# Placing four stores of the second layer and laying out two state arrays row by row, in a two-layer decoder step

## The chip, the cores and the metric

The kernel runs on one core of a Trainium2 chip. The metric is the device time of one execution in microseconds (us); the time before is the median of three runs. A profile of one execution gives, for each engine, when its instructions ran and what released them. Times inside the trace count from the start of its span.

## What is computed

One inference step of a two-layer decoder, for a prompt of 256 tokens and eight sample sequences of one token each; all 264 tokens share the weights. Cut to what matters here:

```python
def sb_pool_mixer(x, pos, past_kv, pool_prev, norm_g, w_in, pool_w, pool_scale, w_out):   # layer 1
    h = rmsnorm(x, norm_g)
    z = h @ w_in
    q, k, v, u = jnp.split(z, [C_WIDTH, 2 * C_WIDTH, 3 * C_WIDTH], axis=-1)
    ...
    new_kv = jnp.stack([k, v], axis=2)
    c_out = stick_breaking_attention(q, k_all, v_all, pos).reshape(B, T, C_WIDTH)
    d_out = pool_mixer(pool_prev, u, pos, pool_w, pool_scale)
    new_pool = jnp.concatenate([pool_prev, u], axis=1)[:, -POOL_STATE:]
    y = jnp.concatenate([c_out, d_out], axis=-1) @ w_out
    return x + y, new_kv, new_pool

def conv_ffn(x, prev, norm_g, w_gate, w_up, conv_w, conv_b, w_down):                       # both layers
    g_all = jnp.concatenate([prev, h @ w_gate], axis=1)
    gc = sum(conv_w[i] * g_all[:, i:i + T] for i in range(CONV_W)) + conv_b
    ...
```

Outputs besides the activations are the new keys and values (k1 and v1 in layer 1), the last 15 pooling inputs of the prompt (poolp) and of the eight samples (pools), and the convolution states. The pooling state of the samples comes in as 15 earlier rows of 512 features for each sequence; a sequence's new state is rows 1 to 14 of these and the new row.

## The kernel before

The features lie on the 128 partitions, the 264 tokens along the free axis. Every weight is cut into blocks of 128 x 128, packed in the order of use, and streamed from device memory in chunks: sixteen blocks, 1 MB, each. A chunk goes into one of three buffers of the pool `rawp` (tile `raw`, issued in `raw`, line 280, through `late`, line 274). `split` (line 292) turns each half chunk, eight blocks, into two operand tiles: `wh` by a copy on ScalarE (ACT, line 300) and the rest `wl` by a subtraction on VectorE (DVE, line 301). It does so three tiles ahead of TensorE (PE), in four buffers. `run` (line 306) then issues three matmuls for each block, 24 for a tile.

The phases follow each other: in0, out0, ff0, dn0 for layer 0, then in1, out1, ff1, dn1. Phase in1 (line 1079) has 128 blocks in the order u, q, k, v, four output tiles of eight blocks each. The other work of the layer hangs on it by block number: `blk(b, f)` calls `f` in the trace after block b. The places that matter:

- `norm1` at block 12, which sets the scale that the evacuations of in1 need; `pool_in` (lines 1022 to 1024) writes `U` and column 15 of `PALL`; `pool_sum` (line 1026) at block 33 copies the tail of `U` to `plp` on GpSimd (POOL, line 1028) and forms the window sums on DVE.
- Sixteen pages of the cached values, 256 KB each, are loaded two at a time from block 40 to block 96 (`drip_of(vload, 2)`); two pages share one tile `V`.
- `zs_score` (line 996) at block 72 multiplies the sample queries with the cached keys (tile `sc`); `stick` (line 958) makes weights of the scores, with two sigmoids on ACT (lines 962, 963) and a scan and a product on DVE (lines 964, 965), into tile `zs`; `zs_tr` (line 1002) at block 82 transposes `zs` on PE into `pP`.
- `z_qk` at blocks 80, 93, 105, 117 does the same for the prompt (tiles `Z`, `keep`, `w`), and `z_tr` at 91, 104, 116 transposes `w` into `pt`. `sample_av` at blocks 100 and 108 uses the `V` tiles (`pv`).

While `fixed[0]` is true, from line 1060 to line 1092, matmuls keep their order in the trace. Everything that goes through `late`, or is pinned with `keep_in_program_order`, also keeps it. All other instructions are placed by a scheduler, engine by engine. The orders of PE, DVE, ACT and POOL are the same in the kernel before and the changed one.

Every weight chunk and every page is issued by SyncE (SP), one after the other. SP waits for a transfer's buffer before it issues it, and what stands behind waits too. Its order in layer 1, from line 935 on, with chunk numbers, is before:

```text
PALL, pw, raw54, raw55, out_pools, out_poolp, V0 V0, raw56, V2 V2 V4 V4, raw57, V6 V6 V8 V8, raw58,
V10 V10, V12 V12, raw59, V14 V14, out_k1, raw60, raw61, out_v1, raw62, raw63
```

Each DMA signals on one of eight semaphores in turn, so that the ninth of a row waits for the first. `PALL` is `[P, 4, 8, 16]` on chip. The load fills its columns 0 to 14 (line 935), and the store `pools` takes columns 1 to 15 (line 1088): 4096 pieces of 60 bytes each way. The convolution state `CSTATE` is `[P, 2, NF, 2, NS]`; `conv_prep` (line 531) stores one of its two rows for each layer, `CSTATE[:, l, :, 1, :]` (line 538), in 2816 pieces of 32 bytes.

Of the kernel before, what the change touches and what calls it, by code (L numbers as in the profile page):

```python
# [9 lines left out]
F32 = mybir.dt.float32  # L10
# [4 lines left out]
ALU = mybir.AluOpType  # L15
# [3 lines left out]
P = 128  # L19
# [3 lines left out]
NS = 8  # L23
T = SEQ + NS
# [7 lines left out]
NF = DFF // P  # L32
# [14 lines left out]
NST = 15  # L47
# [41 lines left out]
def _pack_weights(w_in0, w_out0, w_in1, w_out1, gate, up, down):  # L89
    def blocks(w):  # L90
        kt, mt = w.shape[0] // P, w.shape[1] // P
        return w.reshape(kt, P, mt, P).transpose(2, 0, 1, 3).reshape(mt * kt, P, P), kt

    mats = {"in0": w_in0, "out0": w_out0, "in1": w_in1, "out1": w_out1}
    for l in range(2):
        mats[f"g{l}"], mats[f"u{l}"], mats[f"dn{l}"] = gate[l], up[l], down[l]
    base, kts, parts, n = {}, {}, [], 0
    for name, w in mats.items():
        b, kts[name] = blocks(w)
        base[name] = n  # L100
        parts.append(b)
        n += b.shape[0]
    allb = np.concatenate(parts)
    idx = []
    for ph, order in _PHASES:
        for (n_, t), k in order:
            if ph in _COLS:
                name, m = ph, _COLS[ph][n_] + t
            elif ph.startswith("ff"):
                name, m = n_ + ph[2], t  # L110
            else:
                name, m = ph, t
            idx.append(base[name] + m * kts[name] + k)
    out, o = [], 0
    for c in _CHUNKS:
        out.append(allb[np.array(idx[o:o + c])].transpose(1, 0, 2).reshape(-1))
        o += c
    return out
# [11 lines left out]
def _pack_first(gain, x, chunks):  # L130
    w = np.concatenate([c.reshape(P, -1) for c in chunks[:2]], 1)
    rows = []
    for i, ((b, e), (m, n)) in enumerate(_FIRST):
        rows.append(np.concatenate(([gain] if i == 0 else []) + [w[:, b * P:e * P], x[:, m:n].reshape(P, -1)], 1).reshape(-1))
    return np.concatenate(rows)
# [18 lines left out]
def _consts():  # L154
# [35 lines left out]
_INS = [  # L190
    ("w", ((_NB - 16) * P * P,)), ("xw", (P * (KD + 16 * P + KD * T),)), ("x", (P, KD * T)), ("vec", (P, _NVEC)), ("cst", _CST_ARR.shape), ("rope", (P, 2 * T)),
    ("kt0", (NPHYS, P, 512)), ("vp0", (NPHYS, P, 512)), ("kt1", (NPHYS, P, 512)), ("vp1", (NPHYS, P, 512)),
    ("cstate", (P, 2 * NF * 2 * NS)), ("pstate", (P, 4 * NS * NST)),
    ("sguw", (P, 512)), ("sgub", (P, 512)), ("poolw", (P, 512)),
]
_OUTS = [
    ("y", (KD, P, T)), ("k0", (P, 4, T)), ("v0", (P, 4, T)), ("bvn", (P, 4, NS)),
    ("k1", (P, 4, T)), ("v1", (P, 4, T)), ("poolp", (P, 4, NST)), ("pools", (P, 4, NS, NST)),
    ("cv0", (P, NF, 10)), ("cv1", (P, NF, 10)), ("cs0", (P, NF, NS)), ("cs1", (P, NF, NS)),
]  # L200

# [2 lines left out]
def tile_decoder_step(ctx: ExitStack, tc: tile.TileContext, a):  # L204
    nc = tc.nc
    v, s, g = nc.vector, nc.scalar, nc.gpsimd
# [16 lines left out]
    con = ctx.enter_context(tc.tile_pool(name="con", bufs=1))  # L223
# [8 lines left out]
    def f4(name, shape=(P, 4, T), dt=F32):  # L232
        return up.tile(list(shape), dt, tag="u", name=name)
# [11 lines left out]
    VEC = con.tile([P, _NVEC], F32, name="VEC")  # L245
    CST = con.tile([P, _CST_ARR.shape[1]], F32, name="CST")
    PT = con.tile([1, NS * NPG], I32, name="PT")
    CSTATE = con.tile([P, 2, NF, 2, NS], F32, name="CSTATE")
    C0 = con.tile([P, 2, NF, NS], F32, name="C0")
    PALL = con.tile([P, 4, NS, 16], F32, name="PALL")  # L250

# [4 lines left out]
    def vec(n):  # L256
        o, w = _VEC[n]
        return VEC[:, o:o + w]
# [15 lines left out]
    def late(dst, src):  # L274
        tc.keep_in_program_order(nc.sync.dma_start(dst, src))
# [30 lines left out]
    def run(order, rhs, evac, hooks=None):  # L306
        hooks = sorted((hooks or {}).items())
        n = 0
        seen, left, ps = {}, {}, {}
        for m, k in order:  # L310
            left[m] = left.get(m, 0) + 1
        for m, k in order:
            i = pos[0]
            pos[0] += 1
            h, l = split(i // 8)
            c = (i % 8) * P
            if m not in ps:
                ps[m] = at(f"mm{i}") if i in spare else psm.tile([P, 512], F32, tag="mm", name=f"mm{i}")
                first = True
            else:  # L320
                first = False
            left[m] -= 1
            o = ps[m][:, :T]
            xh, xl = rhs(m, k)
            pe.matmul(o, h[:, c:c + P], xh, start=first, stop=False)
            pe.matmul(o, h[:, c:c + P], xl, start=False, stop=False)
            pe.matmul(o, l[:, c:c + P], xh, start=False, stop=left[m] == 0)
            if left[m] == 0:
                evac(m, o)
            n += 1  # L330
            while hooks and n >= round(8 * (hooks[0][0] + 1)):
                for f in hooks.pop(0)[1]:
                    f()
# [11 lines left out]
    first, o = [], 0  # L345
# [185 lines left out]
    def conv_prep(l):  # L531
        cw = vec("cw")
        w = lambda i: cw[:, (l * 3 + i) * NF:(l * 3 + i + 1) * NF].unsqueeze(2).to_broadcast([P, NF, NS])
        t = sm.tile([P, NF, NS], F32, tag="cprep", name=f"cprep{l}", bufs=1)
        g.tensor_tensor(C0[:, l], CSTATE[:, l, :, 0, :], w(0), ALU.mult)
        g.tensor_tensor(t, CSTATE[:, l, :, 1, :], w(1), ALU.mult)
        g.tensor_tensor(C0[:, l], C0[:, l], t, ALU.add)
        nc.sync.dma_start(a[f"cs{l}"], CSTATE[:, l, :, 1, :])

    def ffn(l, xg, R, down_evac, hooks=None):  # L540
        cw, cb = vec("cw"), vec("cb")
# [61 lines left out]
    def pick(xg):  # L603
        return lambda m, k: hl(xg, k)
# [69 lines left out]
    q4, k4, v4 = f4("q4"), f4("k4"), f4("v4")  # L674
# [187 lines left out]
    blk = lambda b, f, *x: hk.at(b / 8 - 1, f, *x)  # L862
# [51 lines left out]
        blk(8, s_av, t)  # L914


    late(CSTATE, a["cstate"].rearrange("p (l j i s) -> p l j i s", l=2, j=NF, i=2))
    for l in range(2):
        conv_prep(l)

# [11 lines left out]
    ffn(0, xg, R, evac, hk)  # L932


    late(PALL[:, :, :, 0:NST], a["pstate"].rearrange("p (g s i) -> p g s i", g=4, s=NS))
    xg = xg1
    q4, k4, v4 = f4("q4b"), f4("k4b"), f4("v4b")
    vt = f4("vt1", (P, 2, 512))
# [3 lines left out]
    plp = sm.tile([P, 4, NST], F32, tag="plp", name="plp", bufs=1)  # L942
# [118 lines left out]
    blk = lambda b, f, *x: hk.at(b / 8 - 1, f, *x)  # L1061
# [7 lines left out]
        blk(b, z_qk, t)  # L1069
    for t, b in enumerate((91, 104, 116)):  # L1070
        blk(b, z_tr, t)
    blk(100, lambda: nc.sync.dma_start(a["k1"], k4))
    for i, b in enumerate((62, 66, 70, 76)):
        blk(b, pool_mix, i)
    for t, b in enumerate((110, 118, 126)):
# [1 line left out]
    for i, b in enumerate((100, 108)):  # L1077
        blk(b, sample_av_of(st1, PZ, vtiles, i, "l1"))
    run(orders["in1"], pick(xg), in1_evac, hk)
    nc.sync.dma_start(a["v1"], v4)  # L1080
    hk = Hooks()
    blk(1, zs_out)
    blk(2, z_tr, 3)
    blk(6, lambda: v_pair(vt, v4[:, 3, :], 3, "v1"))
    for t in range(4):
        blk(9, z_av, t)
    nc.sync.dma_start(a["poolp"], plp)
    nc.sync.dma_start(a["pools"], PALL[:, :, :, 1:16])

    xg, nrm, evac = residual(vec("f1"), "f1")  # L1090
    run(orders["out1"], pick([catA, catB]), evac, hk)
# [12 lines left out]
def _lay(inp):  # L1104
    f = {n: np.asarray(x) for n, x in inp.items()}
    x = np.concatenate([f["x_prompt"].reshape(SEQ, D), f["x_sample"].reshape(NS, D)])
    col = lambda w: w.reshape(-1, P).T
    kt = lambda c: c[:, :, 0].reshape(NPHYS, P, 4, P).transpose(0, 3, 2, 1).reshape(NPHYS, P, 512)
    vecs = {"n1": col(f["l1_norm"]), "f0": col(f["ffn_norm"][0]), "f1": col(f["ffn_norm"][1]),
            "fin": col(f["final_norm"]), "sg": col(f["l0_sgu_gain"]), "ps": col(f["l1_pool_scale"]),  # L1110
            "cw": col(f["ffn_conv_w"].reshape(-1)), "cb": col(f["ffn_conv_b"].reshape(-1)),
            "w00": np.tile(f["l0_sgu_w"][:, 0, 0][None, :], (P, 1)), "b00": np.tile(f["l0_sgu_b"][:, 0][None, :], (P, 1))}
    ws = _pack_weights(f["l0_w_in"], f["l0_w_out"], f["l1_w_in"], f["l1_w_out"], f["ffn_w_gate"], f["ffn_w_up"], f["ffn_w_down"])
    xt = x.T.reshape(KD, P, T).transpose(1, 0, 2)
    return {
        "w": np.concatenate(ws[2:]),
        "xw": _pack_first(col(f["l0_norm"]), xt, ws),
        "x": xt.reshape(P, KD * T),
        "vec": np.concatenate([vecs[n] for n in _VEC], 1),
        "cst": _CST_ARR,  # L1120
        "rope": _ROPE,
        "kt0": kt(f["cache_l0_kv"]), "vp0": f["cache_l0_kv"][:, :, 1].reshape(NPHYS, P, 512),
        "kt1": kt(f["cache_l1_kv"]), "vp1": f["cache_l1_kv"][:, :, 1].reshape(NPHYS, P, 512),
        "pt": f["page_table"].reshape(1, NS * NPG),
        "cstate": f["state_ffn_conv"].reshape(2, NS, 2, NF, P).transpose(4, 0, 3, 2, 1).reshape(P, -1),
        "pstate": f["state_l1_pool"].reshape(NS, NST, 4, P).transpose(3, 2, 0, 1).reshape(P, -1),
        "sguw": f["l0_sgu_w"].transpose(2, 0, 1).reshape(P, 512),
        "sgub": np.tile(f["l0_sgu_b"].reshape(1, 512), (P, 1)),
        "poolw": f["l1_pool_w"].transpose(1, 0, 2).reshape(P, 512),
    }  # L1130
# [39 lines left out]
```

## Time and profile before

| | us |
|---|---|
| time, median of 3 runs (lowest, highest) | 611.6 (610.9, 612.25) |
| the profiled execution | 612.44 |
| span of its trace | 610.3 |
| PE busy in the span | 593.2 |
| DVE, ACT, POOL busy | 417.4, 343.8, 66.7 |
| mean granted PE clock, share of full speed | 0.994 |

The profiled execution's own time is 2.14 us more than its span, and 0.84 us more than the median of the runs shown. PE is busy for 97% of the span, so a change in any other engine or queue shows in the time only where PE waits for it. Waits of an engine are listed with the instruction that ended them; "SPq" is SyncE's queue of DMA issues, and "landing" is the moment at which all of a transfer has arrived. "DMA" in a table of stretches is the busy share of the 16 DMA engines; it can be over 1, where packets overlap.

### The profile page before, as it was taken

Reading aid. Unit: us, or ns where it says so; the run is one execution under the profiler, and the core shown is the slowest. Engines: PE = TensorE matmul, PEld = TensorE weight load, DVE = VectorE, ACT = ScalarE, POOL = GpSimd, SP = SyncE. Lnnn points to the kernel's source line nnn. Section 1 sums busy time; section 2 is a strip of 40 time slices with the busy share of each in tenths; the row PEclk is TensorE's granted clock in tenths of the full one; section 3 lists DMA queues with packets and bytes.
Section 4 is the critical chain, followed back from the end, with each engine's and each line's share of the span. In section 5 each row is a group of like instructions: output and inputs, shape, how many; then the busy total and the mean of one; then the engine's idle time right before and its main releaser. Section 6 shows DMA issues by size and latency. Waiting matters only on the chain.

```text
span 610.3 us, 12279 instructions
## 1 busy us (share of the span) xinstructions
PE 593.2 (97%) x4908; PEld 573.3 (94%) x4908; DVE 417.4 (68%) x711; ACT 343.8 (56%) x607; POOL 66.7 (11%) x83
## 2 busy tenths in 40 slices
PE   8999999999999999999999799999999999999994
PEld 7988879999999999999999588999999999999994
DVE  6899566879776766655559276597986766754442
ACT  7757755576655555544454256566665555555441
POOL 4100002341000000011110000033300000001120
PEclk9999999999999999999999999999999999999998
DMA  8998936544654554894579992445365454564502
GB/s 324 347 396 293 333 123 173 200 147 139 213 202 164 182 205 150 333 333 166 201 178 86 262 356 106 169 154 198 133 214 177 169 207 158 189 209 154 199 1 71
DMA packets 41258, 122.23 MB, mean 200 GB/s; under 512 B 17138, under 2 KB 18546, under 8 KB 29810
## 3 DMA queue, kind: packets, MB, share of 16 engines
q1 hardware_dynamic: 40368, 120.25, 60.0%
q10 hardware_dynamic: 834, 1.20, 0.6%
q8 instruction: 38, 0.62, 0.4%
q14 instruction: 18, 0.15, 0.1%
HBM read 117.50 MB, written 3.94 MB: 199 GB/s over the span
## 4 chain that ended last, share of the span: by engine, by line
PE 71%; DVE 3%; DMA 2%; issue 1%; ACT 1%; POOL 0%; DVEq 0%; SPq 0%; ACTq 0%
PE mm L216 68%; DMA raw<-in_w 2%; DVE xn_l L386 1%; DVE wl L301 1%; PE pv_l L216 1%; PE Z L216 1%; PE pav L216 0%; DVE wk L565 0%; PE pt L219 0%; DVE X L1100 0%; DVE wk L566 0%; ACT wh L300 0%; POOL wk L576 0%; DVE wk L561 0%; PE vtp_v L219 0%
## 5 line engine op out<-in xcount | busy, mean ns | idle before, releaser
L301 DVE TENSOR_TENSOR wl<-raw,wh 128x1024 fp32r<-128x1024 f32 x179 | 220.4, 1231 | 132.7 <-ACT wh L300 130.8
L300 ACT ACTIVATE wh<-raw 128x1024 fp32r<-128x1024 f32 x179 | 189.6, 1060 | 184.4 <-PE mm L216 164.0
L216 PE MATMUL mm<-xn_h,wh 128*128 128x264 f32 x544 | 154.7, 284 | 0.0
L216 PE MATMUL mm<-xn_l,wh 128*128 128x264 f32 x544 | 154.5, 284 | 0.0
L216 PE MATMUL mm<-xn_h,wl 128*128 128x264 f32 x544 | 153.4, 282 | 0.0
L216 PEld LDWEIGHTS mm<-xn_h,wh 128*128 128x128 f32 x544 | 102.2, 188 | 0.2 <-ACT cvo L568 0.2
L216 PEld LDWEIGHTS mm<-xn_l,wh 128*128 128x128 f32 x544 | 102.2, 188 | 0.0
L216 PEld LDWEIGHTS mm<-xn_h,wl 128*128 128x128 f32 x544 | 102.2, 188 | 0.0
L216 PE MATMUL mm<-a_l,wh 128*128 128x264 f32 x352 | 99.8, 284 | 0.0
L216 PE MATMUL mm<-a_h,wh 128*128 128x264 f32 x352 | 99.7, 284 | 0.0
L216 PE MATMUL mm<-a_h,wl 128*128 128x264 f32 x352 | 99.3, 282 | 0.0
L216 PEld LDWEIGHTS mm<-a_l,wh 128*128 128x128 f32 x352 | 66.1, 188 | 0.0
L216 PEld LDWEIGHTS mm<-a_h,wl 128*128 128x128 f32 x352 | 66.1, 188 | 0.0
L216 PEld LDWEIGHTS mm<-a_h,wh 128*128 128x128 f32 x352 | 66.0, 188 | 0.0
L216 PE MATMUL mm<-xg_h,wh 128*128 128x264 f32 x160 | 48.2, 301 | 1.3 <-ACT xg_h L385 1.3
L216 PE MATMUL mm<-xg_f_h,wh 128*128 128x264 f32 x160 | 46.0, 288 | 2.0 <-DVE wk L575 2.0
L216 PE MATMUL mm<-xg_l,wh 128*128 128x264 f32 x160 | 46.2, 289 | 0.0
L216 PE MATMUL mm<-xg_h,wl 128*128 128x264 f32 x160 | 46.1, 288 | 0.0
L216 PE MATMUL mm<-xg_f_l,wh 128*128 128x264 f32 x160 | 45.4, 284 | 0.0
L216 PE MATMUL mm<-xg_f_h,wl 128*128 128x264 f32 x160 | 45.1, 282 | 0.0
L216 PE MATMUL mm<-xg_n_h,wh 128*128 128x264 f32 x128 | 39.2, 307 | 0.0
L216 PE MATMUL mm<-xg_n_l,wh 128*128 128x264 f32 x128 | 36.9, 288 | 0.0
(249 smaller groups left out, 1055.5 us busy)
## 6 DMA issues: line engine op xcount, KB each, us to landing
raw<-in_w SPq DMA_DIRECT2D x89, 1024.0 KB, 4.9
K<-in_kt SPq DMA_DIRECT2D x32, 256.0 KB, 6.1
V<-in_vp SPq DMA_DIRECT2D x32, 256.0 KB, 7.2
raw<-in_w SPq DMA_DIRECT2D x4, 512.0 KB, 5.8
X<-in_x SPq DMA_DIRECT2D x4, 264.0 KB
xw<-in_xw SPq DMA_DIRECT2D x2, 388.0 KB, 5.6
out_k<-k SPq DMA_DIRECT2D x1, 528.0 KB
out_v<-v SPq DMA_DIRECT2D x1, 528.0 KB
```

The costliest lines, as they stand in the source:

```text
L216: return self.keep(nc.tensor.matmul(*x, **k))
L300: s.activation(h, src, AF.Copy)
L301: v.tensor_tensor(l, src, h.bitcast(F32), ALU.subtract)
L386: j = v.scalar_tensor_tensor(l, src, gain, h.bitcast(F32), ALU.mult, ALU.subtract)
```

## The change

Four things are done. The stores of `poolp` and `pools` leave the trace's end of phase in1, where the scheduler placed them, and are held at block 84 of in1; the store of `k1` is held at block 112 instead of being a free one at block 100; the store of `v1` moves from the end of in1 to block 12 of out1, and is held there. The pooling state is given 16 columns for each sequence in device memory as well (the sixteenth is padding on the way in, and the first is dropped on the host on the way out), so that load and store move whole rows of 2 KB. The convolution state is laid out with its two rows outside the feature blocks, so that the row that is stored is contiguous: 704 bytes for each partition. SP's order in layer 1 after it:

```text
PALL, pw, raw54, raw55, V0 V0, raw56, V2 V2 V4 V4, raw57, V6 V6 V8 V8, raw58, V10 V10, out_poolp,
out_pools, V12 V12, raw59, V14 V14, raw60, out_k1, raw61, raw62, out_v1, raw63
```

```diff
-    ("cstate", (P, 2 * NF * 2 * NS)), ("pstate", (P, 4 * NS * NST)),
+    ("cstate", (P, 2 * NF * 2 * NS)), ("pstate", (P, 4 * NS * 16)),
...
-    ("k1", (P, 4, T)), ("v1", (P, 4, T)), ("poolp", (P, 4, NST)), ("pools", (P, 4, NS, NST)),
+    ("k1", (P, 4, T)), ("v1", (P, 4, T)), ("poolp", (P, 4, NST)), ("pools", (P, 4, NS, 16)),
...
-    CSTATE = con.tile([P, 2, NF, 2, NS], F32, name="CSTATE")
+    CSTATE = con.tile([P, 2, 2, NF, NS], F32, name="CSTATE")
...
-        g.tensor_tensor(C0[:, l], CSTATE[:, l, :, 0, :], w(0), ALU.mult)
-        g.tensor_tensor(t, CSTATE[:, l, :, 1, :], w(1), ALU.mult)
+        g.tensor_tensor(C0[:, l], CSTATE[:, l, 0], w(0), ALU.mult)
+        g.tensor_tensor(t, CSTATE[:, l, 1], w(1), ALU.mult)
         g.tensor_tensor(C0[:, l], C0[:, l], t, ALU.add)
-        nc.sync.dma_start(a[f"cs{l}"], CSTATE[:, l, :, 1, :])
+        nc.sync.dma_start(a[f"cs{l}"], CSTATE[:, l, 1])
...
-    late(CSTATE, a["cstate"].rearrange("p (l j i s) -> p l j i s", l=2, j=NF, i=2))
+    late(CSTATE, a["cstate"].rearrange("p (l i j s) -> p l i j s", l=2, i=2, j=NF))
...
-    late(PALL[:, :, :, 0:NST], a["pstate"].rearrange("p (g s i) -> p g s i", g=4, s=NS))
+    late(PALL, a["pstate"].rearrange("p (g s i) -> p g s i", g=4, s=NS))
...
-    blk(100, lambda: nc.sync.dma_start(a["k1"], k4))
+    blk(84, late, a["poolp"], plp)
+    blk(84, late, a["pools"], PALL)
+    blk(112, late, a["k1"], k4)
...
     run(orders["in1"], pick(xg), in1_evac, hk)
-    nc.sync.dma_start(a["v1"], v4)
     hk = Hooks()
     blk(1, zs_out)
     blk(2, z_tr, 3)
     blk(6, lambda: v_pair(vt, v4[:, 3, :], 3, "v1"))
     for t in range(4):
         blk(9, z_av, t)
-    nc.sync.dma_start(a["poolp"], plp)
-    nc.sync.dma_start(a["pools"], PALL[:, :, :, 1:16])
+    blk(12, late, a["v1"], v4)
...
-    pools = o["pools"].transpose(2, 3, 1, 0).reshape(NS, NST, 512)
+    pools = o["pools"][..., 1:].transpose(2, 3, 1, 0).reshape(NS, NST, 512)
```

More of the change, by code (lines that the diff above doesn't have):

```diff
@@ L1124, in _lay @@
         "pt": f["page_table"].reshape(1, NS * NPG),
-        "cstate": f["state_ffn_conv"].reshape(2, NS, 2, NF, P).transpose(4, 0, 3, 2, 1).reshape(P, -1),
-        "pstate": f["state_l1_pool"].reshape(NS, NST, 4, P).transpose(3, 2, 0, 1).reshape(P, -1),
+        "cstate": f["state_ffn_conv"].reshape(2, NS, 2, NF, P).transpose(4, 0, 2, 3, 1).reshape(P, -1),
+        "pstate": np.pad(f["state_l1_pool"].reshape(NS, NST, 4, P).transpose(3, 2, 0, 1), ((0, 0), (0, 0), (0, 0), (0, 1))).reshape(P, -1),
         "sguw": f["l0_sgu_w"].transpose(2, 0, 1).reshape(P, 512),
```

## The prediction

> **What bounds the kernel now.** I read the page first, for which engine is full.
>
> ```profile
> PE 593.2 (97%) x4908; PEld 573.3 (94%) x4908; DVE 417.4 (68%) x711; ACT 343.8 (56%) x607; POOL 66.7 (11%) x83
> ```
>
> PE works for 593.2 of 610.3 us, and the changed kernel gives it the same instructions in the same order. So all that can be won is time in which PE waits, or runs slowly. Next, therefore, PE's own list of waits (who waited for whom, us in total, times, longest):
>
> ```profile
> PE pP L219 <- DVE zs L965: 3.9, 1, 3.9
> PE mm L216 <- DVE wk L575: 2.0, 2, 1.0
> PE mm L216 <- ACT xg_h L385: 1.3, 1, 1.3
> ```
>
> The list has six rows; the three not shown are smaller still. One wait stands out, a single 3.9 us in layer 1; the others hang on work that the change doesn't touch. The chain that ended last shows what lay behind it (start, us, what):
>
> ```profile
> 333.64 13.46 DMA raw<-in_w
> ...
> 347.20 1.07 ACT wh L300
> ...
> 349.52 0.61 DVE keep_s L964
> ...
> 350.70 0.69 PE pP L219 x2
> 351.39 4.41 PE mm L216 x27
> 355.80 0.66 PE pt L219 x6
> ...
> 367.90 1.85 PE pv_l L216 x16
> ...
> 370.69 0.22 PE vtp_v L219 x2
> 370.91 2.18 PE mm L216 x18
> ```
>
> A weight chunk (chunk 56) took 13.46 us from issue to landing, at 347.10. The copy `wh` waited for it; behind that copy, in ACT's order, stood the sigmoids of the sample scores, and PE's transposes `pP` needed their result. From landing to `pP` it is 350.70 - 347.10 = 3.6 us. PE didn't lack weights: it lacked `zs`.
>
> Why was the chunk late? SP's timeline, one wait of SP's, and the table of stretches (busy PE, PEld, DVE, ACT, POOL, granted clock, DMA share, GB/s):
>
> ```profile
> 322.37 0.58 SPq L1088 DMA_DIRECT2D out_pools<-PALL  x1
> 323.01 7.76 SPq L1087 DMA_DIRECT2D out_poolp<-plp  x1
> 330.97 2.61 SPq L275 DMA_DIRECT2D V<-in_vp  x2
> 333.64 0.42 SPq L275 DMA_DIRECT2D raw<-in_w  x1
> ```
>
> ```profile
> SPq L275 <- DMA out_pools<-PALL: 5.1, 1, 5.1
> ```
>
> ```profile
> 326.00:330.00 4.00, 4.00 (x35) 4.00 (x34) 4.00 (x10) 1.06 (x1) 0.00 (x0) 1.00 2.11 18
> 342.00:346.00 4.00, 4.00 (x33) 3.35 (x32) 0.00 (x0) 0.00 (x0) 0.00 (x0) 1.00 0.92 346
> ```
>
> The store of `pools`, 4096 pieces of 60 bytes, keeps the DMA engines over-full (2.11) while they move 18 GB/s; afterwards they move 346. `out_poolp` behind it takes 7.76 us only to issue, and a page load waits for `out_pools` to land until about 342, some 19.5 us after its issue. So chunk 56 is issued late, and crawls.
>
> **The change, part by part.** *The store of pools and poolp, 12 pages and 3 chunks later, in whole rows.* When could chunk 56 have started? Its buffer is that of chunk 53, free when DVE has read that chunk's second half:
>
> ```profile
> 323.84 1.21 DVE L301 TENSOR_TENSOR wl<-raw,wh 128x1024 fp32r<-128x1024 f32 x1
> 348.29 1.23 DVE L301 TENSOR_TENSOR wl<-raw,wh 128x1024 fp32r<-128x1024 f32 x1 [9.96 <-ACT wh L300]
> ```
>
> These are the second half of chunk 53 and the first half of chunk 56, with four readings (chunks 54 and 55) between them. So the chunk can be issued at 323.84 + 1.21 = 325.05, not 333.64. Before it in SP's queue now stand only two pages, whose buffer came free when dn0 ended, before in1 began. How late may it land?
>
> ```profile
> 337.61 3.66 PE L216 MATMUL sc<-K,qz_l 128*32 128x256 f32 x64
> 344.96 0.93 PE L216 MATMUL Z<-k4b,q4b 64*128 64x128 f32 x8
> 346.53 0.28 PE L216 MATMUL mm<-xg_n_h,wl 128*128 128x264 f32 x1
> ```
>
> PE is ready for `pP` at 346.53 + 0.28 = 346.81 (and 3.89 later it starts), so a landing up to 346.81 - 3.6 = 343.2 costs nothing; 325.05 plus even this chunk's slow 13.46 is 338.5. Removed in full: the wait of 3.89.
>
> *The slow matmuls after the wait.* `pP` and the 27 matmuls behind it take 0.69 + 4.41 = 5.10 us in the chain. The same kinds further on, two transposes in 0.22 and 18 matmuls in 2.18 (0.121 each), give 0.22 + 27 x 0.121 = 3.49. So 1.61 more goes when the wait goes. The granted clock tells why:
>
> ```profile
> 350.00:355.00 5.00, 4.30 (x24) 4.30 (x25) 4.90 (x9) 2.26 (x8) 0.00 (x0) 0.66 1.05 410
> ```
>
> It is 0.66 in this stretch and 1.00 in those above. By the Trainium skill, "TensorE: Matmul & The Clock Gate", Part 1, PE falls to half clock after an idle window of about 3.4 us and needs about as much busy time to come back; the trace agrees, with 3.89 idle and a mean of 0.66. By its figures, as an estimate, the tail costs 3.4 x 0.5 = 1.7 in place of 1.61, and the time would come out 0.1 lower.
>
> *Does another wait come up at once?* The next place is `pt` after block 91, 0.22 + 3.27 us behind 346.81, at 350.3. `Z` ends at 345.89 and needs:
>
> ```profile
> 349.06 1.06 ACT L300 ACTIVATE wh<-raw 128x1024 fp32r<-128x1024 f32 x1
> 350.00 0.50 ACT L962 ACTIVATE keep<-Z 128x384 f32<-128x384 f32 x1
> 352.44 1.80 DVE L964 TENSOR_TENSOR_SCAN keep<-keep,edge 128x384 f32<-128x384 f32 x2
> 354.15 1.00 DVE L965 TENSOR_TENSOR w<-w,keep 128x383 f32<-128x383 f32 x2
> ```
>
> The next `wh` waits for the tile that ends at block 80, where `Z` begins, about 344.7, and ends at 345.8; its `wl` (1.23) ends at 347.1; then scans 1.80 and products 1.00 make 349.9 for both heads. The first head is needed at 350.3, the second 0.33 later (half of 0.66). That is 0.4 to 0.7 us of slack: I take 0, bounds 0 and +1.0, which is another `wh` of 1.06 caught in between. If this cover is gone, `pt` is what is late next.
>
> *Where the stores stand now.* Issued behind the twelfth page of the cache, they follow the score products (337.6 to 341.3) whose buffers the later pages need, so at about 339. Behind them wait six loads of the layer: four pages and chunks 59 and 60. Chunk 59 needs chunk 56's buffer, whose second half DVE ends at 347.1 as above. So SP would stand there anyway, eight us after the stores. `plp` and `PALL` were ready at 322.4, when the old stores went out; the held stores wait for no engine. As 2 KB rows `pools` is of the kind of a 256 KB page. With even chunk 56's slow 13.46 to land, 339 + 13.5 = 352.5. The pages behind are needed by the second `pv`, at 367.90 - 5.5 = 362.4. I take 0, and +1 as the upper bound. `poolp` remains 240-byte pieces: 128 of them, against 4096 in 19.5 us, make 0.6 us of the queues. The Trainium skill, "DMA: Bandwidth & Descriptors", Specifications, puts line rate at 512 bytes a piece, so `poolp` stays below it; on that rule, too, the term off the path is zero.
>
> *k1 and v1.* Each goes behind one chunk more, k1 behind 60, v1 behind 62, with 528 KB either way and one issue each. The weights gain an earlier place, and no wait of PE's stands there (list above): 0. Their buffers are written again only in ff1, the phase after out1.
>
> *Loads and stores of layer 0's end and PALL's load.* The pieces of CSTATE's stores and of PALL's load cost SP and the queues time now:
>
> ```profile
> 94.75 2.15 SPq L538 DMA_DIRECT2D out_cs<-CSTATE  x2
> 306.62 0.64 SPq L275 DMA_DIRECT2D PALL<-in_pstate  x1
> ```
>
> ```profile
> L1024 DVE TENSOR_TENSOR PALL<-mm,R_n x4: 160/164/166, 317.9 to 322.2; 128x8 f32<-128x8 f32 x4
> ```
>
> PE waits for nothing in either place: chunks already landed cover them. So taking them away wins 0 (bounds 0 and 0.3, a few issue gaps). Column 15 of PALL is now written by the load as well, so DVE's first write there must follow the landing. The first of the four writes was at 317.9, 11 us after the issue at 306.62; cost 0.
>
> **Sum.** 612.44 (profiled execution) - 3.89 - 1.61 = 606.94; bounds of the rest -0.3 and +2. The runs shown have their median 0.84 below the profiled execution. If that is a constant, the median becomes 606.1. If it is this very stall, which came out longer in the profiled execution, 606.9. I take the middle, **606.5**; own range 605.5 to 607.9.
>
> **Rivals.**
> 1. *A shorter wait stays.* DVE has little slack at `pt`, or chunk 56 meets six pages on the queues. For it: the 0.4 us of slack. Against: the landing has 4.7 us to spare even at 13.46. A leftover of 1 to 2.5 us gives 607.5 to 609, say 608.2. Chance 0.12. By the Trainium skill ("TensorE: Matmul & The Clock Gate", Part 1) a gap under 3.4 us would leave the clock up, so only the gap itself would be paid.
> 2. *The change doesn't do what it says: SP stood still for pages, not for the store.* Pages do wait for buffers, the later ones for the score products. But none of those stands before chunk 56; only the two of 330.97 do, and they were behind the store. No change, 611.6. Chance 0.03.
> 3. *Slower: the stores clog the queues again, in a worse place.* If the stores take the old 19.5 us from 339, the last pages start at 358.5 and race `pv` at 362.4. It decides when the last page lands after 366.3, for then the new gap, with its 1.6 of slow clock, eats the 5.5 won. A landing at 368 gives 612.44 - 5.5 + 5.6 + 1.6 = 614.1, or 613.3 by the median. For it: stores have shown that they can. Against: 128 pieces in place of 4096. Chance 0.03.
>
> **How the numbers follow.** Forecast 0.82, rivals 0.12, 0.03, 0.03. The range reaches from 605.1 (the sum by the median, 606.1, less 0.3 and the 0.7 from the median down to the lowest run) over the forecast's and the first rival's times to 608.8. Within 0.2% (1.2 us, about what this measurement can tell) is 610.4 to 612.8: rival 2, and a little of rival 1. Faster 0.93, same 0.04, slower 0.03.
>
> **What would show it.** In the changed kernel's profile: PE's wait for `zs` gone; no stretch near 350 with a clock under 1; chunk 56 issued near 325 and landed before 340; the DMA share near 1 or below from 322 to 340; span near 604.8. Wrong: a PE wait at `pt` or `pv` in place of the old one, or chunk 56 still issued after 330. If the span falls by 5.5 while chunk 56 lands late, the account of the path is wrong although the number is right.

## The result and the profile after

| | before | after |
|---|---|---|
| median, us (lowest to highest, runs) | 611.92 (610.9 to 613.54, 4) | 606.14 (605.47 to 606.86, 4) |
| ratio, 95% interval | | 0.9903 [0.9878, 0.9928] |
| the profiled execution, and its span | 612.44, 610.3 | 606.86, 604.8 |

The change takes 5.8 us off the median. The page of the changed kernel, its first line and the one that counts packets:

```profile
PE 591.5 (98%) x4908; PEld 571.9 (95%) x4908; DVE 417.7 (69%) x711; ACT 344.3 (57%) x607; POOL 66.9 (11%) x83
...
DMA packets 27946, 122.26 MB, mean 202 GB/s; under 512 B 3314, under 2 KB 4978, under 8 KB 16498
```

As many matmuls as before, in a span 5.5 us shorter. Before, 41258 packets were moved, 17138 of them under 512 bytes; now 3314 are. PE's list of waits, whole (us in total, times, longest):

```profile
PE mm L216 <- DVE wk L575: 2.0, 2, 1.0
PE S L216 <- DVE k L692: 1.3, 1, 1.3
PE warm L216 <- DVE warm L371: 1.2, 1, 1.2
PE mm L216 <- ACT xg_h L385: 0.9, 1, 0.9
PE ns_fin L216 <- ACT sq_fin L398: 0.6, 1, 0.6
```

The row of `pP` waiting for `zs`, 3.9 us before, is gone, and nothing has taken its place; the others differ by 0.4 us at most. SP's timeline says why:

```profile
325.06 0.34 SPq L275 DMA_DIRECT2D raw<-in_w  x1
325.60 2.06 SPq L275 DMA_DIRECT2D V<-in_vp  x4
...
340.82 0.37 SPq L275 DMA_DIRECT2D out_poolp<-plp  x1
341.25 0.42 SPq L275 DMA_DIRECT2D out_pools<-PALL  x1
341.92 0.88 SPq L275 DMA_DIRECT2D V<-in_vp  x2
```

Chunk 56 is issued at 325.06 in place of 333.64, and lands 4.9 us later in place of 13.46. The stores take 0.37 and 0.42 us of SP, where `out_poolp` alone took 7.76, and `pools` lands 5.8 us after its issue instead of some 19.5. On ACT, the copy of chunk 56 and the two sigmoids behind it:

```profile
337.57 1.06 ACT L300 ACTIVATE wh<-raw 128x1024 fp32r<-128x1024 f32 x1
341.31 0.38 ACT L962 ACTIVATE keep_s<-sc 128x256 f32<-128x256 f32 x1 [2.68 <-PE sc L216]
341.59 0.38 ACT L963 ACTIVATE zs<-sc 128x256 f32<-128x256 f32 x1
```

The copy no longer waits for a transfer; the sigmoids wait for the scores alone, and are done almost 7 us earlier. The chain now runs through PE without a break (start, us, what), and two stretches show the rest (busy PE, PEld, DVE, ACT, POOL, granted clock, DMA share, GB/s):

```profile
345.86 0.93 PE mm L216 x6
...
347.01 3.28 PE mm L216 x27
350.29 0.65 PE pt L219 x6
...
362.38 1.85 PE pv_l L216 x16
```

```profile
326.00:330.00 4.00, 4.00 (x36) 4.00 (x35) 4.00 (x10) 1.06 (x1) 0.00 (x0) 1.00 0.94 332
350.00:355.00 5.00, 5.00 (x44) 4.41 (x43) 2.74 (x4) 3.19 (x8) 0.00 (x0) 1.00 0.51 200
```

The 27 matmuls behind `pP` take 3.28 us where they took 4.41, and the clock in 350 to 355 is 1.00 where it was 0.66. The DMA engines carry 332 GB/s where the short pieces left 18.

### The profile page after: what moved, and what is told of

Its sections match the earlier page's. It is cut to its first block, busy times and chain, and to the rows that moved or that the text cites. A ratio compares the mean times of both kernels' runs of the same rounds, so it can differ in the third digit from the quotient of the medians.

```text
span 604.8 us, 12275 instructions
## 1 busy us (share of the span) xinstructions
PE 591.5 (98%) x4908; PEld 571.9 (95%) x4908; DVE 417.7 (69%) x711; ACT 344.3 (57%) x607; POOL 66.9 (11%) x83
## 2 busy tenths in 40 slices
DMA packets 27946, 122.26 MB, mean 202 GB/s; under 512 B 3314, under 2 KB 4978, under 8 KB 16498
## 4 chain that ended last, share of the span: by engine, by line
PE 73%; DVE 3%; issue 1%; ACT 1%; POOL 0%; DVEq 0%; ACTq 0%
PE mm L216 70%; DVE xn_l L386 1%; PE Z L216 1%; PE pv_l L216 1%; PE sc L216 1%; PE pav L216 0%; DVE wk L565 0%; PE pt L219 0%; DVE wl L301 0%; DVE X L1100 0%; PE pm L216 0%; DVE wk L566 0%; POOL wk L576 0%; DVE wk L561 0%; PE vtp_v L219 0%
```

## The experiments

Each run was compared with runs of the kernel before on the same chip, whose median differs from chip to chip and from time to time (609.97 to 613.51 us). So the ratio counts, not the difference of medians taken at different times.

**The place alone.** On the kernel before, so with the old layouts:

```diff
-    blk(100, lambda: nc.sync.dma_start(a["k1"], k4))
+    blk(84, late, a["poolp"], plp)
+    blk(84, late, a["pools"], PALL[:, :, :, 1:16])
+    blk(112, late, a["k1"], k4)
...
-    nc.sync.dma_start(a["v1"], v4)
...
-    nc.sync.dma_start(a["poolp"], plp)
-    nc.sync.dma_start(a["pools"], PALL[:, :, :, 1:16])
+    blk(12, late, a["v1"], v4)
```

> The four stores are placed as in the change, but pools keeps its 4096 pieces of 60 bytes and all states keep their old layout. Theory (the store hurt only because chunk 56 stood behind it): pools is issued near 341 and takes the old 19.5 us, to about 361; chunk 56 is issued at 325 and PE's wait for zs is gone. The pages behind (needed at 362.4) and chunk 59 land late but in time: 606 to 607.5 us, PE waits of 0 to 1 us in phase in1. Rival (the pieces matter wherever they stand): a new wait of PE at the second pv or at a weight tile behind it, 2 to 7 us, 608 to 614 us.

Measured: 613.32 us, ratio 1.0007 [0.9986, 1.0029]. No gain; the theory missed and the rival held. PE's first wait, SP's queue behind the store, and the chain:

```profile
PE pv_l L216 <- DMA V<-in_vp: 4.0, 2, 2.8
```

```profile
341.46 0.69 SPq L275 DMA_DIRECT2D out_pools<-PALL  x1
342.41 11.71 SPq L275 DMA_DIRECT2D V<-in_vp  x2
354.23 0.46 SPq L275 DMA_DIRECT2D raw<-in_w  x1
354.93 2.57 SPq L275 DMA_DIRECT2D V<-in_vp  x2
```

```profile
354.93 13.71 DMA V<-in_vp
368.64 0.04 issue
368.68 3.34 PE pv_l L216 x10
```

The first wait did go: chunk 56 left at 325.28 and landed 5.0 us later. But the store took 22.4 us to land, and so did the page issued next, at 342.41; issuing two pages behind the store took 11.71, and the first of the last two pages, issued at 354.93, landed at 368.64. PE reached the second `pv` at 362.55 and left it at 372.02: 9.47 us where the changed kernel needs 1.85. That is 7.6 us of the 7.9 by which its span, 612.7, exceeds 604.8. (The list counts 4.0 of the 9.47 as waiting. The sixteen matmuls take the other 5.4; the granted clock was 0.90 from 365 to 370 and 0.76 from 370 to 375, and the ends of matmuls are modelled, so the profile doesn't divide this further.) The stall had moved, from the weights to the pages.

**The rows alone.** The changed kernel with the four stores put back (the diff above, inverted, and `PALL` stored whole):

> Both new layouts, but the four stores stand where the scheduler placed them before. Theory: pools in 128 rows of 2 KB, issued at 322.4, lands within 6 us; poolp no longer blocks; chunk 56 is issued by 326 and lands by 333; the wait for zs is gone: 606.1 us, as the whole change. Rival (the place in the queue matters by itself): SP still stands behind the stores, chunk 56 comes after 330 and a wait of 1 to 4 us stays: 608 to 612 us.

Measured: 606.5 us, ratio 0.9882 [0.9842, 0.9922]. SP's timeline:

```profile
322.15 0.34 SPq L1088 DMA_DIRECT2D out_pools<-PALL  x1
322.55 0.42 SPq L1087 DMA_DIRECT2D out_poolp<-plp  x1
323.17 1.62 SPq L275 DMA_DIRECT2D V<-in_vp  x2
324.86 0.40 SPq L275 DMA_DIRECT2D raw<-in_w  x1
```

In its old place, ahead of the pages and of chunk 56, the store now takes SP 0.34 us and lands in 3.8. The whole gain is there without moving anything.

**The pooling state alone, and the convolution state alone.** The first takes from the change only `pstate` and `pools` with 16 columns; the second only this:

```diff
-    CSTATE = con.tile([P, 2, NF, 2, NS], F32, name="CSTATE")
+    CSTATE = con.tile([P, 2, 2, NF, NS], F32, name="CSTATE")
...
-        nc.sync.dma_start(a[f"cs{l}"], CSTATE[:, l, :, 1, :])
+        nc.sync.dma_start(a[f"cs{l}"], CSTATE[:, l, 1])
```

> Only the pooling state has the new layout; the convolution state and the places of the stores are those of before. Theory: everything that is won hangs on the store of pools: 606.1 us. Rival (the shorter stores of the convolution state win a part): 0.5 to 2 us more than the run with both layouts.

> Only the convolution state has the new layout. Theory: its two stores at 95 us land sooner, but PE waits for nothing there; the wait of 3.9 us for zs stays: no change, 611 to 612.5 us. Rival: 0.5 to 2 us faster.

Measured: the pooling state alone 606.52 us, ratio 0.9888 [0.9849, 0.9928], the same as with both layouts. The convolution state alone 611.43 us, ratio 0.9975 [0.9957, 0.9993]: a small gain where none was expected. So it was measured again, and a third time beside a control, the kernel before against itself:

> The same kernel as conv_rows_only, which came out at a ratio of 0.9975 where no change was expected. Theory (that stall differs from run to run, and 60-byte stores set it): ratio within 0.998 to 1.002 here. Rival (the shorter convolution stores win something by themselves): 0.996 to 0.998 again, with pools landing sooner than in the runs of before.

> The kernel before, unchanged, measured against itself, beside conv_rows_third on the same chip. Expected: ratio 1.000 within its interval of about 0.2%; pools lands after 17 to 20 us, and PE waits 2 to 5 us for zs. If the ratio lies outside 0.998 to 1.002, the measure itself has an error of the size of the result for the convolution state.

> The kernel of conv_rows_only once more. Theory A (the shorter convolution stores make the later store of pools land sooner, while it is still in pieces): ratio 0.996 to 0.998 again, pools lands 1 to 2 us sooner than in before_itself. Theory B (the two results before were chance, the stall differs between executions): ratio 0.998 to 1.002, and pools lands in the same time as in before_itself.

Measured: 0.9963 [0.9941, 0.9986] the second time, as the rival had it. The third time it was 0.9986 [0.9971, 1.0], beside a control of 0.9991 [0.9972, 1.001]. PE's wait in the control, and in the three profiles of the convolution state alone, in order:

```profile
PE pP L219 <- DVE zs L965: 3.4, 1, 3.4
```

```profile
PE pP L219 <- DVE zs L965: 2.5, 1, 2.5
```

```profile
PE pP L219 <- DVE zs L965: 2.0, 1, 2.0
```

```profile
PE pP L219 <- DVE zs L965: 2.8, 1, 2.8
```

The wait of one and the same kernel differs from execution to execution: the one shown before the change had 3.9, the control has 3.4. `pools` landed 17.8 to 18.4 us after its issue in the three, and 19.0 and some 19.5 in the two of the kernel before. A sooner landing needs no convolution rows, though: in late_zs below, on another chip but with every DMA of the kernel before, `pools` landed in 17.3. Beside the control, the convolution rows show no gain; the two times before they do. So it stays open whether they shorten that stall by up to 2 us while `pools` is in pieces. With `pools` in rows they win nothing (606.5 against 606.52).

**Fewer pieces.** The pooling state in 16 columns, but part of it stored as before, at the old place; n is 2 or 3 of the four groups:

```diff
-    nc.sync.dma_start(a["pools"], PALL[:, :, :, 1:16])
+    nc.sync.dma_start(a["pools"][:, :n, :, 1:16], PALL[:, :n, :, 1:16])
+    nc.sync.dma_start(a["pools"][:, n:], PALL[:, n:])
```

> Stores where they were before; two of the four groups of pools go out in 2048 pieces of 60 bytes, the other two in rows of 1 KB. Theory (a threshold: chunk 56 may land until 343.2): the pieces take about 9.7 us, chunk 56 lands near 338, between the 347.1 of before and some 330 without pieces; PE does not wait: 606.1 us. Rival (cost in proportion to the pieces): half of the gain, 609 us.

> As the run before it, with 3072 pieces of 60 bytes and one group in rows of 512 bytes. Theory: chunk 56 lands near 342.8, just at the threshold; PE waits 0 to 0.5 us, and the clock stays up: 606 to 606.8 us. Rival (proportion): a quarter of the gain, 610.5 us.

Measured, with 609.97 us for the kernel before: half the pieces 607.16, ratio 0.9956 [0.9943, 0.997]; three quarters 606.73, ratio 0.9944 [0.9927, 0.9961]. The rival's times were worked out from a slower kernel before. On this chip nearly the whole change gains 3.6 us (kv_as_before, below), so a cost in proportion to the pieces would have given some 608.2 and 609.1. No wait for `zs` in either profile. With three quarters:

```profile
326.31 0.43 SPq L1087 DMA_DIRECT2D out_poolp<-plp  x1
327.32 3.97 SPq L275 DMA_DIRECT2D V<-in_vp  x2
331.40 0.37 SPq L275 DMA_DIRECT2D raw<-in_w  x1
```

```profile
338.79 1.06 ACT L300 ACTIVATE wh<-raw 128x1024 fp32r<-128x1024 f32 x1 [0.65 <-DMA raw<-in_w]
```

Chunk 56 lands at 331.40 + 7.3 = 338.7, ACT waits 0.65 us for it, and PE not at all. It is a threshold and no proportion. (With half, the pieces went out at 319.6, 2.8 us sooner than in the kernel before, because the two groups were ready by then. The median is 0.8 us above that of kv_as_before, but the profiled spans are both 604.9, so no profile shows where those 0.8 lie.) The landing of three quarters was expected at 342.8, though. These pieces landed in about 11 us, 3.6 ns each, against 4.8 for the 4096; they begin 64 bytes apart in device memory, those of before 60 apart. Whether that is why wasn't tried.

**Does PE lack weights, or zs?** The DMAs of before, with two pieces of PE's work later:

```diff
-    blk(82, zs_tr)
+    blk(92, zs_tr)
...
-    for t, b in enumerate((91, 104, 116)):
+    for t, b in enumerate((100, 104, 116)):
         blk(b, z_tr, t)
```

> All DMAs, layouts and the order of SP are those of before; only the PE work that waits for the stick weights is moved back in the trace: zs_tr from block 82 to 92, the first z_tr from 91 to 100. Theory (PE lacked zs, not weights): chunk 56 still lands near 347, but PE has weights until block 96 and goes on; a wait of 0.2 to 1.2 us is left (a PSUM bank that DVE empties late), the clock stays up: 606.8 to 608 us. Rival (PE stands because the weights are late): the wait of about 4 us only moves to the next weight tile, 610.5 to 612.5 us.

Measured: 606.99 us, ratio 0.9954 [0.9936, 0.9973], beside 606.37, ratio 0.9939 [0.9921, 0.9957], for the run below, which has nearly the whole change, on the same chip. ACT's row for chunk 56 and PE's chain:

```profile
348.39 1.06 ACT L300 ACTIVATE wh<-raw 128x1024 fp32r<-128x1024 f32 x1 [8.03 <-DMA raw<-in_w]
```

```profile
348.77 4.56 PE mm L216 x36
353.33 0.22 PE pP L219 x2
```

The copy still waits 8.03 us for the transfer, and PE works straight through into `pP`. (This execution came to layer 1 some 2.9 us later than the others; `out_pools` went out at 325.25. The delay is in layer 0 and is looked at in the last section.) PE had weights enough; what it lacked was `zs`, which stood behind the copy in ACT's order.

**k1 and v1.** The change with these two stores where they were before:

> The change, but with the stores of k1 and v1 where they were before. Theory: worth nothing, 606.1 us. Rival: the chunk that stands behind k1 or v1 is late and 0.5 to 2 us come back.

Measured: 606.37 us, ratio 0.9939 [0.9921, 0.9957]. In other measurements the whole change had 606.14 and the rows alone 606.5. Nothing comes back. (In this profile `pools`, in the place of the change and in rows, took 1.84 us to issue and 7.6 to land, so rows vary too.)

**Pieces where nobody waits.** The kernel before, with the store of `pools` moved to the end of the last phase, still in 4096 pieces:

```diff
-    nc.sync.dma_start(a["pools"], PALL[:, :, :, 1:16])
...
-    ffn(1, xg, R, evac)
+    hk = Hooks()
+    hk.at(122 / 8 - 1, late, a["pools"], PALL[:, :, :, 1:16])
+    ffn(1, xg, R, evac, hk)
```

> The kernel before, with one edit: the store of pools, still in 4096 pieces of 60 bytes, is held behind the last weight chunk, in the last phase, where the DMA engines had nothing to do for some 25 us. Theory (the pieces cost only what is queued behind them and needed within 20 us): issued near 575, landed by 597, ahead of the stores of y at about 599 (5.5 earlier than before): the whole gain, 606 to 607 us, or the time of before less 3 to 6 us on this chip. Rival (4096 short writes cost wherever they stand, so place_only was no matter of place): 609 us and more.

Measured: 606.94 us, ratio 0.9893 [0.985, 0.9937]. SP's last rows and a stretch:

```profile
569.41 0.59 SPq L275 DMA_DIRECT2D out_pools<-PALL  x1
599.05 2.57 SPq L1102 DMA_DIRECT2D out_y<-X  x3
```

```profile
575.00:580.00 5.00, 5.00 (x44) 5.00 (x43) 1.82 (x2) 2.12 (x2) 0.43 (x1) 1.00 1.99 18
```

The store is as slow as ever, 20.7 us to land, with the DMA engines over-full at 18 GB/s, and it costs nothing: behind it come only the stores of `y`, nine us after it has landed. So the right place alone would have done it as well; the place of the change, with pieces, does not.

## Why the prediction was right

1. *Only PE's waits and slow matmuls could be won.* Right: same instructions, span shorter by the 3.89 and the 1.61 us of the sum. The second `pv` starts at 362.38 in place of 367.90, so 5.52 us are won in that one place. The span was put near 604.8, and is 604.8; that it fits so closely is partly luck, for two waits in other places, for `k` and `xg_h`, moved by 0.4 us up and down and cancel.
2. *The chain from store to chunk 56 to ACT to zs.* Shown: late_zs breaks it at its last link, with the chunk as late as ever, and rows_only and tail_pieces at its first.
3. *Chunk 56 could go at 325.05, and may land until 343.2.* It went at 325.06 and landed at 330.0. Landings at 338.2 (half the pieces) and 338.7 cost PE nothing. Past the bound PE waits, as shown below the list.
4. *No new wait at pt.* Right, with DVE's products at 349.64 in time for 350.13. The small slack is real: in the second run of the convolution state alone, where `pP` waited 2.0, PE waited another 0.4 us at `pt` for DVE.
5. *The stores in their new place cost nothing.* Right for rows, and the row layout is what makes it so. Issue at 340.8 and 341.3 against the 339 of the text, landing in 5.8. The bound of that step, 352.5, was made for rows, and for rows it held: 347.1 here, and 349.2 in kv_as_before. Pieces break it: place_only shows 22.4 us to land, and pages that land at 364.8 and 368.6. That is the third rival's mechanism, with its place (the second `pv`) and nearly its price: it had put a landing at 368, and the time 1.7 us above that of before, where 0.7 was measured, inside the interval of no change. It took the pieces to bring it about.
6. *k1, v1, the convolution stores, the load of PALL: nothing.* Right in the presence of the row store. tail_pieces, which still loads `PALL` in pieces, has the whole gain, so that load costs nothing that these runs can tell. For the convolution stores beside a store in pieces it is open, as told above.
7. *606.5 as the middle of 606.1 and 606.9.* Measured 606.14, beside a profiled execution of 606.86, 0.72 above its median. So the two readings of the offset come out as 606.1 by a constant, which was right here, and 606.9 by the stall, which was not; the middle was a choice and not a reason, and with four runs the 0.72 can be chance. The stall's own length varies too, from 3.4 to 3.9 us in two profiles of the kernel before. The kernel before spreads over 610.1 to 617.2 us on two chips and 608.2 to 611.3 on a third; the kernels without the stall mostly stay within 605.5 to 607.

The bound of step 3 can be read where chunk 56 was later than that. Its rows in the control, and in the first and second run of the convolution state alone (issue, us to landing):

```profile
333.14 13.50 DMA raw<-in_w
```

```profile
331.74 14.09 DMA raw<-in_w
```

```profile
331.94 13.36 DMA raw<-in_w
```

These landings, 346.6, 345.8 and 345.3, and the 347.1 before the change, less PE's waits of 3.4, 2.5, 2.0 and 3.9, all give 343.2 to 343.3. (The third run of the convolution state came to layer 1 some 0.9 us sooner, so its times don't compare.) What comes later than the bound, PE waits for in full.

## What to carry to other kernels

In these runs a store cost what its pieces made the queue do, not what its bytes are: 240 KB in pieces of 60 bytes took 17 to 22 us to land, as 2 KB rows 3.8 to 7.6. Before moving such a store, look at what is queued behind it in the next 20 us and when that is needed; a place is good if none of it is needed before the store has landed. And where a transfer ends a chain, ask which instruction behind the waiting one, on the same engine, is what the busy engine lacks: moving that one can hide the transfer without touching it.

## What the runs showed of the hardware that was not expected

The slow clock came after short gaps. Gaps of 2.5 and 2.8 us (the convolution state alone, first and third run) were followed by a granted clock of 0.76 and 0.73 in the stretch of 350 to 355, and one of 2.0 us (second run) by 1.00. In order, the stretches:

```profile
350.00:355.00 5.00, 5.00 (x35) 5.00 (x35) 4.83 (x8) 1.83 (x5) 0.00 (x0) 0.76 1.03 404
```

```profile
350.00:355.00 5.00, 5.00 (x33) 5.00 (x33) 4.66 (x7) 1.67 (x3) 0.00 (x0) 0.73 1.03 404
```

```profile
350.00:355.00 5.00, 4.59 (x38) 3.99 (x36) 4.84 (x7) 2.11 (x4) 0.00 (x0) 1.00 1.04 405
```

So the prediction's first rival was wrong to let a gap under 3.4 us keep the clock: at 2.5 and 2.8 us, in these runs, it did not. The Trainium skill, "TensorE: Matmul & The Clock Gate", Part 1, puts the idle window at about 3.4 us; these gaps are shorter.

Nor does the length of the gap alone decide. In layer 0 of late_zs, PE waited 1.9 us for `k`, where it waited 0.9 before the change, and half clock followed; together these make most of that execution's 2.9 us. The wait, and two stretches of 3.41 us:

```profile
PE S L216 <- DVE k L692: 1.9, 1, 1.9
```

```profile
38.24:41.65 3.41, 1.54 (x14) 1.19 (x14) 3.41 (x8) 1.58 (x3) 0.00 (x0) 1.00 1.05 410
41.65:45.06 3.41, 3.41 (x18) 3.41 (x17) 2.39 (x10) 2.13 (x9) 0.00 (x0) 0.50 1.00 396
```

With three quarters of the pieces the same wait was 2.0 us, and the clock stayed at 1.00. In each of the six traces with half clock in mid-kernel it lasts 3.41 us, and PE was idle for 1.9 to 3.4 us of the 3.41 just before it. Counted in such steps, the two gaps of 2.0 us that kept the clock are split, into 0.4 and 1.6 us and into 1.2 and 0.8. That would fit a clock set step by step from how idle the step before was; no run was made to test it.

Short pieces also differ among themselves. Before the change the two stores of the convolution state, 2816 pieces of 32 bytes each, landed in 4.1 and 5.5 us, 1.5 to 2 ns a piece; the 60-byte pieces of `pools` took 4.8. As rows, the convolution stores land in 1.6 to 1.7 us.
